# Hybrid decoder trunk on one core: pool mixer features moved directly behind the keys, memory sums queued later, one accumulator bank of the values in another pool

## The chip, the core and the metric

The kernel runs on one core of a Trainium2 chip. The metric is the device time of one execution in microseconds, the median of several runs. The core has a matrix engine (TensorE, PE in the rows), VectorE (DVE), ScalarE (ACT), GpSimd (POOL), SyncE (SP), whose queue issues most of the transfers, and 16 DMA engines. Each engine works through its own queue in order, and engines meet at semaphores.

## What is computed

One decoder layer for 256 tokens of width 2048, all in float32:

- a mixer on the normalized input `h`: eight heads of a gated DeltaNet (width 1024) beside a multi-scale pool mixer (width 1024), both out of one projection `p = h @ w_in`, then an output projection;
- cross-attention into 256 memory tokens, with keys and values from `mem_h @ w_xkv`;
- a gated MLP with a causal convolution, and a final norm.

The pool mixer, of which this is about, is short:

```python
for i, w in enumerate((2, 4, 8, 16)):           # four groups of 256 features
    mean = (running sum of u over the last w positions) / min(position, w)
    groups.append(mean - u)
y = einsum('bsng,ngh->bsnh', stack(groups), w_pool) * pool_scale
```

The DeltaNet takes q, k, v, z out of the same projection (q, k, v through a causal convolution of 4 taps and SiLU), builds for each head and each half of the tokens a triangular matrix from the keys, inverts it, and runs two chunks of 128 tokens through the state.

## The kernel before

Activations are kept transposed (features on partitions, 256 tokens along the row). Every float32 product is made of three: weights and activations are split in a high and a low part (`split`, lines 100 to 102: ScalarE copies the high part, VectorE subtracts), and high x high, high x low and low x high are accumulated. `gemm_part` (lines 132 to 146) does one feature tile of 128 outputs with 16 pairs of matmuls, one of 512 columns and one of 256.

`unit` (line 126) gives a gemm its weights: `load_raw` fetches 1 MB on SP's queue into one of three `raw` buffers, and `wsplit` splits it in two halves, each into one of four `whi` and `wlo` buffers. So the split of weights can run two gemms ahead of TensorE.

**Order of the work.** The text of the kernel is not the order of the engines: a planner sorts the instructions by the place in the text and by its own reckoning of when each is ready, and keeps the dependencies. `tc.issue_after(x)` ties what is written inside to come behind `x` on the engine of `x`. Side work is written as generators in lanes. `pump(anchor)` is called three times in each gemm (line 145, behind k-tiles 4, 9 and 15); it advances every lane by one step and ties that step's matmuls behind the gemm's own matmul. The lanes are "dn" (decays, four key pairs, inverses), "dp" (the four delta pairs, one after the other), "pool" (outputs of the pool groups) and "mem" (the memory tokens).

The stage around the change, lines 640 to 839, in the order of the text:

1. eight key features `in_k` with their convolution (lines 640 to 648); behind each second one a `key_pair` joins lane "dn"; then `inverses`;
2. four pairs p = 0 to 3 of heads (lines 651 to 666): two q, two v, two z projections; q and v go through `conv_feature` (evacuation, a scaling on GpSimd at line 347, one ScalarE step at 349, three VectorE steps at 351), then `delta_pair(p)` joins lane "dp"; behind pair 1 the lane "mem" gets `memory()`;
3. four pool groups (line 667): `pool_group` (lines 580 to 607) loads `w_pool[n]`, splits it, does two projections `in_u`, scales each on GpSimd (592), sums windows on GpSimd with n+1 additions (598), forms the mean on VectorE (602 to 605), splits it into `mx`, and queues `pool_out` (567 to 579), which waits 6+n steps and then multiplies by the weights and writes rows of yT;
4. sixteen memory keys `kk` (830 to 839). Behind key 0 lane "mem" is drained, behind key 8 lanes "dn", "dp" and "pool", and `memory_sums` (674 to 694) joins lane "ms": for two thirds of the memory features sums and differences of the token halves, split into `mS`, needed by the memory values;
5. the memory values (`values`, 696 to 825), a Strassen-like scheme with seven products b1 to b7, each in a bank of PSUM. Two pools of banks serve this stage: `psg` with three (the gemms') and `psd` with four.

`inverses` (390 to 451): it sends the key matrices U through DRAM (393, 397) into a layout W of 16x16 blocks, inverts those by 15 times two VectorE steps on V (404, 406), sends V through DRAM into Yall (408, 411), waits 20 steps, and then does for each pair two rounds of a doubling (`Z` on VectorE at 420, `qp` on TensorE two steps later at 425, `pp` two steps later at 432, the subtraction from Yall at 433) and a last round.

`delta_pair` (453 to 565): after SiLU and transposes it waits until the inverse of its pair is done (495), then `wps`, the state, `cps` (520), R on VectorE (524), two steps later `w` (531), then the outputs `ops` (539), their statistics, and five steps later the transposes `otp` (560). Pair 3 has extra waiting steps (`more`).

The steps that the rows name are these lines:

```python
for l in range(2):                                    # inverses
    Z = st4("Z", "sq"); dve.transpose(Z, Y[p]); yield; yield
    pe.matmul(qp[:, j], C[:, j], Z[:, j], ...)         # 425
while not inv_done[p]: yield                           # delta_pair, 495
dve.tensor_tensor(am, mg[:, :, 0], mg[:, :, 1], ALU.add)   # memory_sums, 682
```

Of the kernel before, what the change touches and what calls it, by code (L numbers as in the profile page):

```python
# [10 lines left out]
F32 = mybir.dt.float32  # L11
F32R = mybir.dt.float32r
AF = mybir.ActivationFunctionType
ALU = mybir.AluOpType
# [3 lines left out]
P = 128  # L18
D = 2048
T = 256  # L20
M = 256
KT = D // P
# [20 lines left out]
def hybrid_trunk(ctx, tc, a, out):  # L43
    nc = tc.nc
    act, dve, pool, pe = nc.scalar, nc.vector, nc.gpsimd, nc.tensor
# [3 lines left out]
    psg = pre.enter_context(tc.tile_pool(name="psg", bufs=3, space=bass.MemoryType.PSUM))  # L49
    psd = pre.enter_context(tc.tile_pool(name="psd", bufs=4, space=bass.MemoryType.PSUM))  # L50
# [4 lines left out]
    def big(name, shape, dt):  # L55
        return per.tile(shape, dt, name=name, tag="big", bufs=3)

    def ev(name, n=T):
        return per.tile([P, n], F32, name=name, tag="ev", bufs=4)
# [29 lines left out]
    def pv(k, i=None, j=None):  # L89
        s, e = PRM[k]  # L90
        if i is None:
            return prm[:, s:e]
        return prm[:, s + i:s + (i + 1 if j is None else j)]

    def cv(k):
        s, e = CST[k]
        return cst[:, s:e]


    def split(hi, lo, src):  # L100
        act.copy(hi, src)  # L101
        return dve.tensor_tensor(lo, src, hi.bitcast(F32), ALU.subtract)  # L102
# [10 lines left out]
    last_split = [None]  # L113
# [18 lines left out]
    def gemm_part(ps, u, src, k0, n, tot):  # L132
        i = None
        for k in range(n):
            kk = k0 + k
            h, l = u(k)
            xt = src(kk)
            full = xt.rearrange("p s t -> p (s t)")
            if kk == tot - 1:
                pe.matmul(ps[:, T:], l, xt[:, 0, :], start=False, stop=False)  # L140
                i = pe.matmul(ps, h, full, start=False, stop=True)
            else:
                pe.matmul(ps, h, full, start=kk == 0, stop=False)  # L143
                i = pe.matmul(ps[:, T:], l, xt[:, 0, :], start=False, stop=False)  # L144
            if kk % 16 in (4, 9, 15):
                pump(i)
# [51 lines left out]
    with tc.tile_pool(name="dn", bufs=1, reuse_waits="tile") as dn:  # L198
# [35 lines left out]
        for c in range(4):  # L234
# [5 lines left out]
            if c % 2 == 1:  # L240
                g = c // 2
# [325 lines left out]
        def pool_out(n, mx, wp):  # L567
            for _ in range(6 + n):
                yield
            for o_ in range(2):  # L570
                wu = lambda k: (wp[:, 0, k, o_ * P:(o_ + 1) * P], wp[:, 1, k, o_ * P:(o_ + 1) * P])
                ps = psd.tile([P, 512], F32, name="pool", tag="d")
                gemm_part(ps, wu, lambda k: mx[k], 0, 2, 2)
                f = n * 2 + o_
                c = ev("pc")
                act.activation(c, ps[:, T:], AF.Copy, scale=pv("pool_scale", f))
                yt = ev("py")
                dve.scalar_tensor_tensor(yt, ps[:, :T], pv("pool_scale", f), c, ALU.mult, ALU.add)
                split(yT[:, f, 0, :], yT[:, f, 1, :], yt)

        def pool_group(n):
            wpr = load_raw(a["w_pool"][n], [P, 2, 256], "wp")
            wp = dn.tile([P, 2, 2, 256], F32R, name="wp", tag="u4", bufs=2)
            split(wp[:, 0], wp[:, 1], wpr)
            mx = [dn.tile([P, 2, T], F32R, name="mx", tag="C", bufs=2) for _ in range(2)]
            for c in range(2):
                f = n * 2 + c
                ps = gemm([unit(a["w_in"][f], "wi")], hsrc, [KT], "in_u")
                m = evac(ps, "u")
                A = dn.tile([P, T + 16], F32, name="pA", tag="xp", bufs=3)  # L590
                pool.memset(A[:, 0:16], 0.0)
                pool.tensor_tensor(A[:, 16:], m, rxb, ALU.mult)
                src = A
                for l in range(n + 1):
                    s = 1 << l
                    lo = 2 * s - 1
                    B = dn.tile([P, T + 16], F32, name="pB", tag="xp", bufs=3)
                    pool.tensor_tensor(B[:, lo:], src[:, lo:], src[:, lo - s:T + 16 - s], ALU.add)
                    src = B
                w = 2 << n  # L600
                mt = ev("mt")
                dve.scalar_tensor_tensor(mt, src[:, 16:], 1.0 / w, A[:, 16:], ALU.mult, ALU.subtract)
                m16 = dn.tile([P, 16], F32, name="m16", tag="m16", bufs=1)
                dve.tensor_tensor(m16, src[:, 16:32], cv("inv")[:, n * 16:(n + 1) * 16], ALU.mult)
                dve.tensor_tensor(mt[:, 0:16], m16, A[:, 16:32], ALU.subtract)
                split(mx[c][:, 0, :], mx[c][:, 1, :], mt)
            job("pool", pool_out(n, mx, wp))
# [39 lines left out]
            if h % 2 == 1:  # L647
                job("dn", key_pair(h // 2))
        job("dn", inverses())
        yT = None  # L650
        for p in range(4):
            q2, v2, z2 = (dn.tile([P, 2, T], F32, name=n, tag=n, bufs=b) for n, b in (("q2", 2), ("v2", 1), ("z2", 2)))
            for nm, fb, comp, dst in (("q", 8, 0, q2), ("v", 24, 2, v2)):
                for i in range(2):
                    h = 2 * p + i
                    ps = gemm([unit(a["w_in"][fb + h], "wi")], hsrc, [KT], "in_" + nm)
                    conv_feature(ps, comp, h, dst[:, i, :], "c" + nm)
            for i in range(2):
                ps = gemm([unit(a["w_in"][32 + 2 * p + i], "wi")], hsrc, [KT], "in_z")
                m = evac(ps, "z")  # L660
                pool.tensor_tensor(z2[:, i, :], m, rxb, ALU.mult)
            if yT is None:
                yT = big("yT", [P, KT, 2, T], F32R)
            job("dp", delta_pair(p, q2, v2, z2))
            if p == 1:
                job("mem", memory())
        for n in range(4):
            pool_group(n)
        mT = mbox[0]


# [2 lines left out]
        def memory_sums():  # L674
            for g in range(2):
                tmp = dn.tile([P, 2, 4, T], F32, name="mtmp", tag="kall", bufs=1)
                place = (("Dm0", "Dm1", "Dm2", "Dm3"), ("q2", "q2", "z2", "z2"))[g]
                s = [dn.tile([P, 2, T], F32R, name="mS", tag=n, bufs=1 + g) for n in place]
                mS.append((s[:2], s[2:]))
                am, ss = tmp[:, 0], tmp[:, 1].rearrange("p w (k t) -> p w k t", k=2)  # L680
                mg = mT[:, 4 * g:4 * g + 4]
                dve.tensor_tensor(am, mg[:, :, 0].bitcast(F32), mg[:, :, 1].bitcast(F32), ALU.add)
                yield
                a11, a12, a21, a22 = (am[:, k:k + 2, t * P:(t + 1) * P] for t in range(2) for k in (0, 2))
                s5, s6, s7, s3 = (ss[:, w] for w in range(4))
                dve.tensor_tensor(s5, a21, a22, ALU.subtract)
                dve.tensor_tensor(s7, a11, a21, ALU.subtract)
                yield
                dve.tensor_tensor(s6, a11, s5, ALU.subtract)
                dve.tensor_tensor(s3, a12, s6, ALU.subtract)  # L690
                yield
                for w in range(2):
                    split(s[w], s[2 + w], tmp[:, 1, 2 * w:2 * w + 2])
                yield

        def values():
# [74 lines left out]
            def multiply(c, kind, h, uses):  # L771
                hi, lo = ready.pop((c, kind, h))
                g = int(kind[1]) if kind[0] in "ul" else h
                for name, stat in uses:
                    begins = (c, name) not in bk
                    if begins:
                        pool_, tag = (psg, "g") if name in ("b7", "b2") else (psd, "d")
                        bk[c, name] = pool_.tile([P, 512], F32, name="pvs", tag=tag)
                    ends = h == 1 and ENDS[name] == kind
                    ps = bk[c, name]  # L780
                    for i in range(2):
                        xh, xl = stat(g, i)
                        seq(pe.matmul(ps, xh, hi[:, i], start=begins and i == 0, stop=False, skip_group_check=True))  # L783
                        seq(pe.matmul(ps, xh, lo[:, i], start=False, stop=False, skip_group_check=True))
                        seq(pe.matmul(ps, xl, hi[:, i], start=False, stop=ends and i == 1, skip_group_check=True))  # L785
# [88 lines left out]
    r2, _, r2run = rnorm(sq2, "r2", False)  # L874
# [315 lines left out]
    for s in range(-AHEAD, len(plan)):  # L1190
# [13 lines left out]
        b, k = s // NS, s % NS  # L1204
# [52 lines left out]
    for m, (k, c) in enumerate(steps):  # L1257
# [4 lines left out]
        n = blocks.index(k // 4)  # L1262
# [122 lines left out]
```

## Time and profile before

| | |
|---|---|
| median of three runs | 1519.69 us (1519.25 to 1519.73) |
| the profiled execution | 1517.59 us |
| its span, first to last instruction | 1515.8 us |
| TensorE busy | 98% of the span |
| VectorE, ScalarE, GpSimd busy | 75%, 57%, 15% |
| mean granted TensorE clock | 0.994 |

The span of the stage in question goes from about 77 us (end of the keys) to about 410 us (end of the memory keys); the values follow to about 490 us, and then the output projection, the attention and the MLP, which the change does not touch. A row of the trace says who waited for whom; "idle" is the time in which the engine did nothing ahead of the instruction. Matmuls are pipelined: one of 512 columns is listed with some 0.39 us but the next starts about 0.23 us behind it, so a full TensorE shows as busy without holes.

### The profile page before, as it was taken

How to read it: one execution, taken by the hardware profiler on the slowest of the kernel's cores; microseconds unless marked ns; L12 is line 12 of the kernel's file. 1: busy time of each engine (PE TensorE's matmuls, PEld its weight loads, DVE VectorE, ACT ScalarE, POOL GpSimd, SP SyncE). 2: the span in 40 equal slices, each digit the busy share in tenths (PEclk: the TensorE clock that was granted, in tenths of full speed). 3: DMA queues.
4: the chain of work that ended last, by engine and by line, in shares of the span. 5: the costliest groups of instructions: out<-in, count | busy, mean ns of one | idle time of the engine just before them, and what ended most of it. 6: DMA issues, size and time to landing. Idle time of an engine off the chain costs nothing.

```text
span 1515.8 us, 20595 instructions
## 1 busy us (share of the span) xinstructions
PE 1479.2 (98%) x7698; PEld 1253.6 (83%) x7698; DVE 1137.3 (75%) x1489; ACT 870.9 (57%) x1265; POOL 230.6 (15%) x249
## 2 busy tenths in 40 slices
PE   7899999999999999999999999999999999999997
PEld 5788889888877888998888888888888887888885
DVE  6878887677688776666767898889889998455445
ACT  6565666554466544555656766666666766444433
POOL 0432523442100121000322000000000000000000
PEclk9999999999999999999999999999999999999999
DMA  7345443455476655434569988888888879765651
GB/s 269 123 172 189 142 171 126 144 183 208 157 232 222 249 191 176 163 139 139 195 197 344 285 243 248 256 264 257 266 270 270 247 200 363 242 194 190 196 185 56
DMA packets 74933, 317.07 MB, mean 209 GB/s; under 512 B 12240, under 2 KB 12624, under 8 KB 59728
## 3 DMA queue, kind: packets, MB, share of 16 engines
q1 hardware_dynamic: 67136, 287.96, 54.1%
q0 software_dynamic: 7552, 27.27, 9.6%
q8 instruction: 60, 0.98, 0.3%
q10 hardware_dynamic: 144, 0.52, 0.1%
q14 instruction: 41, 0.34, 0.1%
HBM read 306.15 MB, written 9.57 MB: 208 GB/s over the span
## 4 chain that ended last, share of the span: by engine, by line
PE 81%; DVE 8%; ACT 4%; POOL 3%; DMA 3%; issue 2%; SPq 0%; POOLq 0%; DVEq 0%; ACTq 0%
PE b L1028 10%; PE b L1030 10%; PE b L1029 10%; PE acc L1246 5%; PE acc L1247 5%; PE acc L1248 5%; PE xq L143 4%; PE mix L143 4%; PE xo L143 3%; PE kk L143 3%; PE xq L144 2%; PE mix L144 2%; PE xo L144 2%; PE pvs L783 2%; PE pvs L785 2%
## 5 line engine op out<-in xcount | busy, mean ns | idle before, releaser
L1111 ACT CAST wh<-wr 128x1024 fp32r<-128x1024 f32 x162 | 168.4, 1050 | 87.5 <-DVE wr L1147 30.2
L1112 DVE TENSOR_TENSOR wl<-wr,wh 128x1024 fp32r<-128x1024 f32 x162 | 194.7, 1218 | 26.3 <-ACT wh L1111 25.1
L1028 PE MATMUL b<-wh,hP 128*128 128x512 f32 x484 | 190.8, 395 | 2.4 <-DVE xres L853 2.4
L1030 PE MATMUL b<-wh,hP 128*128 128x512 f32 x484 | 190.3, 394 | 0.0
L1029 PE MATMUL b<-wl,hP 128*128 128x512 f32 x484 | 188.8, 390 | 0.0
L1112 DVE TENSOR_TENSOR wl<-wd,wh 128x1024 fp32r<-128x1024 f32 x88 | 107.5, 1224 | 102.8 <-ACT wh L1111 102.7
L1111 ACT CAST wh<-wd 128x1024 fp32r<-128x1024 f32 x88 | 92.7, 1054 | 118.5 <-PE acc L1248 114.6
L1246 PE MATMUL acc<-wh,aring 128*128 128x512 f32 x320 | 124.5, 389 | 0.0
L1248 PE MATMUL acc<-wh,aring 128*128 128x512 f32 x320 | 124.5, 389 | 0.0
L1247 PE MATMUL acc<-wl,aring 128*128 128x512 f32 x320 | 124.5, 389 | 0.0
L1111 ACT CAST wh<-ring 128x1024 fp32r<-128x1024 f32 x80 | 83.2, 1051 | 53.6 <-PE b L1030 29.4
L1112 DVE TENSOR_TENSOR wl<-ring,wh 128x1024 fp32r<-128x1024 f32 x80 | 96.7, 1218 | 21.4 <-ACT wh L1111 21.4
L102 DVE TENSOR_TENSOR wil<-wi,wih 128x1024 fp32r<-128x1024 f32 x78 | 99.9, 1287 | 15.8 <-ACT wih L101 15.4
L1028 PEld LDWEIGHTS b<-wh,hP 128*128 128x128 f32 x484 | 91.0, 188 | 21.6 <-issue 2.7
L1030 PEld LDWEIGHTS b<-wh,hP 128*128 128x128 f32 x484 | 90.9, 188 | 18.5
L1029 PEld LDWEIGHTS b<-wl,hP 128*128 128x128 f32 x484 | 91.0, 188 | 18.0
L1144 POOL DMA_DIRECT2D ring<-in_w_gu x40 | 34.6, 865 | 379.4 <-DVE sg L1078 365.2
L101 ACT CAST wih<-wi 128x1024 fp32r<-128x1024 f32 x78 | 81.4, 1049 | 17.2 <-DMA wi<-in_w_in 6.3
L143 PE MATMUL xq<-h2T,wqh 128*128 128x512 f32 x240 | 84.9, 393 | 0.0
L143 PE MATMUL kk<-mT,wkh 128*128 128x512 f32 x240 | 84.5, 393 | 0.0
L143 PE MATMUL xo<-oT,woh 128*128 128x512 f32 x240 | 84.3, 392 | 0.0
L143 PE MATMUL mix<-yT,wmh 128*128 128x512 f32 x240 | 84.1, 392 | 0.0
(500 smaller groups left out, 3825.9 us busy)
## 6 DMA issues: line engine op xcount, KB each, us to landing
wr<-in_w_gu SPq DMA_DIRECT2D x158, 512.0 KB, 7.0
wd<-in_w_down SPq DMA_DIRECT2D x88, 512.0 KB, 4.8
wi<-in_w_in SPq DMA_DIRECT2D x39, 1024.0 KB, 4.9
ring<-in_w_gu POOLq DMA_DIRECT2D x40, 512.0 KB, 7.3
wk<-in_w_k SPq DMA_DIRECT2D x16, 1024.0 KB, 4.9
wm<-in_w_mix SPq DMA_DIRECT2D x16, 1024.0 KB, 5.0
wq<-in_w_xq SPq DMA_DIRECT2D x16, 1024.0 KB, 4.9
wo<-in_w_xo SPq DMA_DIRECT2D x16, 1024.0 KB, 4.9
```

The source lines that it names most:

```text
L101: act.copy(hi, src)
L102: return dve.tensor_tensor(lo, src, hi.bitcast(F32), ALU.subtract)
L143: pe.matmul(ps, h, full, start=kk == 0, stop=False)
L144: i = pe.matmul(ps[:, T:], l, xt[:, 0, :], start=False, stop=False)
L1028: pe.matmul(ps, xh, wh, start=first and i == 0, stop=False, skip_group_check=True)
L1029: pe.matmul(ps, xh, wl, start=False, stop=False, skip_group_check=True)
L1030: m = pe.matmul(ps, xl, wh, start=False, stop=last and i == 1, skip_group_check=True)
L1111: cast[:] = [put(act.copy(h, src))]
L1112: less[:] = [put(dve.tensor_tensor(l, src, h.bitcast(F32), ALU.subtract))]
L1246: pe.matmul(acc[t, n], ah, wh, start=first, stop=False)
L1247: pe.matmul(acc[t, n], ah, wl, start=False, stop=False)
L1248: return pe.matmul(acc[t, n], al, wh, start=False, stop=last)
```

## The change

Three edits. The four pool groups go ahead of the pairs, with yT allocated ahead of them; their buffers move to tags that the pairs use later (`wp` in two tiles under the tags of q2 and z2, two buffers each, in place of one tile under `u4`; `mx` under the tags of R and vs, one buffer each, in place of two under `C`). The first operation of each half of the memory sums is tied behind the split of weights that was traced last. The accumulator b6 of the values comes from pool `psg` in place of `psd`.

```diff
@@ pool_out
-                wu = lambda k: (wp[:, 0, k, o_ * P:(o_ + 1) * P], wp[:, 1, k, o_ * P:(o_ + 1) * P])
+                wu = lambda k: (wp[0][:, k, o_ * P:(o_ + 1) * P], wp[1][:, k, o_ * P:(o_ + 1) * P])
@@ pool_group
-            wp = dn.tile([P, 2, 2, 256], F32R, name="wp", tag="u4", bufs=2)
-            split(wp[:, 0], wp[:, 1], wpr)
-            mx = [dn.tile([P, 2, T], F32R, name="mx", tag="C", bufs=2) for _ in range(2)]
+            wp = [dn.tile([P, 2, 256], F32R, name="wp", tag=g, bufs=2) for g in ("q2", "z2")]
+            split(wp[0], wp[1], wpr)
+            mx = [dn.tile([P, 2, T], F32R, name="mx", tag=g, bufs=1) for g in ("R", "vs")]
@@ the stage
         job("dn", inverses())
-        yT = None
+        yT = big("yT", [P, KT, 2, T], F32R)
+        for n in range(4):
+            pool_group(n)
         for p in range(4):
...
-            if yT is None:
-                yT = big("yT", [P, KT, 2, T], F32R)
             job("dp", delta_pair(p, q2, v2, z2))
             if p == 1:
                 job("mem", memory())
-        for n in range(4):
-            pool_group(n)
@@ memory_sums
-                dve.tensor_tensor(am, mg[:, :, 0].bitcast(F32), mg[:, :, 1].bitcast(F32), ALU.add)
+                with tc.issue_after(last_split[0].ins):
+                    dve.tensor_tensor(am, mg[:, :, 0].bitcast(F32), mg[:, :, 1].bitcast(F32), ALU.add)
@@ values, multiply
-                        pool_, tag = (psg, "g") if name in ("b7", "b2") else (psd, "d")
+                        pool_, tag = (psg, "g") if name in ("b7", "b2", "b6") else (psd, "d")
```

## Rows read from the trace of the kernel before

**Rows 1.** The page, part 1: engine, busy us (share of the span), instructions.
```profile
PE 1479.2 (98%) x7698; PEld 1253.6 (83%) x7698; DVE 1137.3 (75%) x1489; ACT 870.9 (57%) x1265; POOL 230.6 (15%) x249
```

**Rows 2.** Waits of TensorE: us in total, times, longest us.
```profile
PE gps L313 <- DVE gg L306: 3.0, 1, 3.0
PE qp L425 <- DVE Z L420: 2.7, 2, 1.5
...
PE w L531 <- DVE R L524: 2.5, 2, 1.4
...
PE otp L560 <- DVE o L554: 2.4, 1, 2.4
PE in_k L143 <- ACT wih L101: 1.4, 1, 1.4
...
PE pvs L783 <- DVE KV L799: 0.5, 2, 0.3
```

**Rows 3.** Windows: the header names the columns; gemms 1 to 8 are 76.6:128.4.
```profile
core 0: us, PE busy (x) PEld busy (x) DVE busy (x) ACT busy (x) POOL busy (x), PEclk, DMA share, GB/s
40.00:50.00 10.00, 7.27 (x42) 6.11 (x41) 9.27 (x30) 4.73 (x9) 3.98 (x6) 1.00 0.28 105
50.00:60.00 10.00, 9.75 (x47) 8.36 (x48) 9.37 (x21) 5.12 (x9) 3.11 (x3) 0.83 0.34 114
76.60:128.40 51.80, 51.80 (x324) 46.38 (x323) 40.71 (x91) 30.14 (x72) 18.60 (x19) 1.00 0.52 171
145.00:350.00 205.00, 197.33 (x1271) 174.33 (x1270) 157.69 (x288) 122.55 (x276) 81.61 (x90) 1.00 0.44 157
252.00:311.00 59.00, 59.00 (x381) 52.62 (x381) 41.47 (x91) 36.32 (x87) 22.47 (x29) 1.00 0.40 136
```

**Rows 4.** Timeline of TensorE: start us, us, instruction [idle before, released by].
```profile
150.07 1.13 PE L425 MATMUL qp<-Z,C 128*128 128x128 f32 x8 [1.11 <-DVE Z L420]
...
161.42 1.13 PE L425 MATMUL qp<-Z,C 128*128 128x128 f32 x8 [1.55 <-DVE Z L420]
...
191.07 0.46 PE L531 MATMUL w<-R,Yall 128*128 128x128 f32 x2 [1.40 <-DVE R L524]
...
320.97 0.49 PE L531 MATMUL w<-R,Yall 128*128 128x128 f32 x2 [1.10 <-DVE R L524]
...
343.46 0.92 PE L560 MATMUL otp<-cst,o 128*128 128x128 f32 x4 [2.37 <-DVE o L554]
```

**Rows 5.** Timeline of VectorE: first, two middle and last of V's steps.
```profile
121.96 0.17 DVE L404 SCALAR_TENSOR_TENSOR tmp<-V,W 128x15 f32<-128x15 f32 x1
...
125.19 0.73 DVE L406 TENSOR_TENSOR V<-V,tmp 128x60 f32<-128x60 f32 x1
...
130.60 0.22 DVE L406 TENSOR_TENSOR V<-V,tmp 128x60 f32<-128x60 f32 x1
...
135.59 0.18 DVE L406 TENSOR_TENSOR V<-V,tmp 128x15 f32<-128x15 f32 x1
```

**Rows 6.** Timeline of SP's queue: V's way back from DRAM.
```profile
139.70 3.77 SPq L411 DMA_DIRECT2D Yall<-vscr  x8
```

**Rows 7.** Timeline of VectorE: what stands ahead of the late steps.
```profile
160.18 0.47 DVE L106 SCALAR_TENSOR_TENSOR mT<-mraw,prm,mT 128x256 fp32r<-128x256 f32 x1
...
187.25 3.41 DVE L351 SCALAR_TENSOR_TENSOR q<-cqxp,prm,q 128x256 f32<-128x256 f32 x6
...
317.75 1.22 DVE L682 TENSOR_TENSOR mtmp<-mT 128x1024 f32<-128x1024 f32 x1
...
319.15 1.50 DVE L102 TENSOR_TENSOR wkl<-wk,wkh 128x1024 fp32r<-128x1024 f32 x1
...
338.10 1.21 DVE L682 TENSOR_TENSOR mtmp<-mT 128x1024 f32<-128x1024 f32 x1
```

**Rows 8.** DMA issues: count, KB each, median us from issue to landing.
```profile
wp<-in_w_pool SPq DMA_DIRECT2D x4, 256.0 KB, 2.9
```

**Rows 9.** Timeline of GpSimd: the scaling of a q feature beside V.
```profile
125.11 0.74 POOL L347 TENSOR_TENSOR cqxp<-cqm,rxrb 128x256 f32<-128x256 f32 x1 [5.93 <-DVE cqm L160]
```

**Rows 10.** Groups of GpSimd, 84 to 345 us: count, busy us, mean ns, idle before.
```profile
L598 POOL TENSOR_TENSOR pB<-pB 128x269 f32<-128x269 f32 x6 | 3.8, 635 | 0.5
```

## The prediction

> **What bounds the kernel now.** I read the page first: TensorE is busy 98% of the span [rows 1], so a change of order that leaves the matmuls alone can only win back TensorE's idle time, or add to it. Next I read TensorE's waits [rows 2]. In the stretch that the change reorders (from the last key feature to the first third of the memory keys) three lines wait: the inverses' `qp` (2.7 us, twice), the delta pairs' `w` (2.5, twice) and `otp` (2.4, once), 7.6 us together. The other long waits (`gps` and its kind) lie ahead of the change or far behind it. So this change is worth 7.6 us at most, 0.5% of the run, plus fractions of a microsecond. About 0.2%, 3.04 us, is what a measurement of this kernel can tell from no change. A wait can also cost more than its length: `gps` waits 3.0 us in the slice 40 to 50, and in the slice behind it the granted clock averages 0.83 [rows 2, 3], a time at the lower of the two levels (1.2 of 2.4 GHz); 17% of 10 us is 1.7 us. The five waits of the stretch are 1.10 to 2.37 us long [rows 4] and lie where the clock is at its upper level [rows 3].
>
> **What moves, counted in pumps.** Lanes advance one step at each of three matmuls per projection, so I number pumps from the end of the keys, three to a gemm, and count yields. The inverses' first real step, `Z` of pair 0, is pump 33, its `qp` pump 35, the second `qp` 39, and pair p's inverse is done at 45+12p: lane "dn" alone sets these, before and after. What runs beside them changes. Before: pairs at gemms 1 to 24, pool features at 25 to 32, memory at pumps 37 to 62; delta pairs end at 56, 70, 84 and 109. After: pool features at gemms 1 to 8, pairs at 9 to 32, memory at pumps 61 to 86; delta pairs start at 43, 61, 79 and 97 and end at 57, 75, 93 and 122. Every pair now finds its inverse done, and pair 3 ends inside memory key 8, just ahead of the drain there, which therefore has nothing to force. The sums start at pump 124 in both.
>
> **The waits one by one**, each from the row before it:
>
> First `qp`, 1.11 us [rows 4]. `Z` needs the inverses' V, which goes through DRAM; V's last step is at 135.59 and SP issues the way back from 139.70 on for 3.77 us [rows 5, 6]. After, the conv features of pairs 0 and 1 no longer run beside V, but pool features do. Bounds: 1.11 gained, or all of rival 2 lost. I take 0.6 gained, the half, because the pool features bring other work.
>
> Second `qp`, 1.55 us [rows 4]. `Z` stands behind a memory split (`mT`, 160.18) and a weight split on VectorE [rows 7]. After, pump 39 is in pair 0 and the memory starts 22 pumps later. Gained: 1.55 (bounds 0 and 1.55).
>
> `w` of pair 0, 1.40 us [rows 4]: R waits behind six conv steps that took 3.41 us [rows 7], in the memory's time. After, this step is pump 51, without memory. Gained: 1.40 (bounds 0 and 1.40).
>
> These two can come back where the memory now runs: beside pairs 2 and 3, inverses 2 and 3 and the deltas of pairs 1 and 2, much the same mix. Bounds: nothing, or both in full, 2.95 us. I take half, 1.5 lost.
>
> `w` of pair 3, 1.10 us [rows 4]. Ahead of R, VectorE did the first operation of the memory sums (1.22 us at 317.75) and between the two R's a weight split of 1.50 [rows 7]. The sums' text comes 24 pumps later, but the planner pulled the operation forward as soon as `kall` was free. The change queues it behind the last weight split traced at pump 124, and R is then at pump 109: it cannot come first. Gained: 1.10 (bounds 0 and 1.10; the split may still stand there).
>
> `otp`, 2.37 us [rows 4]: the sums' second operation (1.21 us at 338.10) stands ahead of the statistics that `otp` needs [rows 7]. After, sums start 2 pumps behind `otp`. Their cost is 1.21, and the rest of the wait is GpSimd's and VectorE's queue. Gained: 2.37 less 0.5 that I leave for that queue (bounds 1.21 and 2.37). Who waits for the sums: `22` of the values, 15 pumps or more behind; cover of that length hides their delay, and without it their four splits would show.
>
> Weights in the pool stage. The four `w_pool` loads (256 KB, 2.9 us to landing [rows 8]) move up on SP past 24 weight loads, and each holds one of three raw buffers until group n-2 has left its `wp` buffers; at the same time SP carries the inverses' trips through DRAM. In the old place SP was free of these. Nothing waits in gemms 1 to 8 now: TensorE is busy 51.80 of 51.80 us [rows 3]. Nearest row: the one wait of a projection for a weight, 1.4 us [rows 2]. Bounds 0 and 1.4; I take 0.5, since the split buffers hold two gemms. The two `memT` loads go back on SP with the memory, beside the same kind of loads as now: nothing.
>
> Edits at nothing: the new tags. `mx` had two buffers and has two, `wp` two and two; the pair's q2 needs group 2's `wp`, read at pump 28, and is written behind gemm 9 (pump 27) after GpSimd's step; R and vs are wanted from pump 45, eight behind the last pool output. Bank b6 from one pool to the other: the projections' pool has three banks, b2 and b7 take two, the third was evacuated with the last memory key. The wait of the values, 0.5 us in two [rows 2], is for a read of b7 and stays (bounds: 0.5 either way).
>
> **Sum.** 0.6 + 1.55 + 1.40 + 1.10 + 1.87 = 6.5 gained; 1.5 + 0.5 = 2.0 lost; net 4.5. The profiled execution took 1517.59 (span 1515.8 and 1.8 around it) and would take 1513.1. The median of the runs is 2.1 above it, 1519.69, so I forecast **1515.2**. With every gain at its upper bound and no loss it is 7.6 less, 1512.1.
>
> **Rival 1: the waits follow the memory.** All three early waits (1.11 + 1.55 + 1.40 = 4.06) are VectorE's queue, and it is the memory with a conv stage that fills it. Then they return in pairs 2 and 3, and only 1.10 + 1.87 - 0.5 = 2.5 us is won: 1517.2, within 0.2%. For it: the same work meets the same chains. Against it: the pairs no longer wait for their inverse, so two of the chains have lost their neighbours.
>
> **Rival 2, on the other side: pool features stop V.** A step of V takes 0.22 us, but the one at 125.19 took 0.73 and ended with the GpSimd operation that had begun at 125.11 and took 0.74 [rows 5, 9]. Undisturbed, eight features hold GpSimd for 8 x 0.74 and 20 sums of 0.635 [rows 9, 10]: 18.6 us in eight gemms, where the eight projections now there have 8 x 0.74 = 5.9. VectorE is already busy 40.71 of 51.80 us there [rows 3], against 41.47 of 59.00 us in the pool features' present place with the deltas. Groups 2 and 3, which meet V, have 14 sums and four scalings in four gemms, 8.9 and 3.0 us, 11.9 of half the 51.80: 46%. If V's 13.8 us (121.96 to 135.77 [rows 5]) stretch by that share, 6.3 us, `qp` waits 1.1 + 6.3 = 7.4 us where I left 0.5, and the clock falls, 1.7: -4.5 + (7.4 - 0.5) + 1.7 = 4.1 slower, 1523.8. It decides from the point where V ends so late that its way back (7.7 us from V's last step to the last of the eight issues [rows 5, 6], and the landing) ends behind pump 33. Against it: keys' U may reach V earlier, as ScalarE no longer waits for conv features ahead of it, and four more pool outputs lie before that pump.
> The Trainium skill (SBUF — State Buffer, section Who interferes with whom) states the rule: a VectorE instruction with two SBUF inputs and a GpSimd instruction that reads SBUF exclude each other for their whole length. By that rule every pool sum that meets a step of V holds it up to the sum's end, and the time is this rival's; the row of 0.73 agrees with it for one pair of operations, and how many pairs meet no run here shows yet.
>
> **A rival that I exclude:** that the change does not do what it says. Text order binds the matmuls (each lane step is tied to a matmul), and the sums to a split; only VectorE's and ScalarE's order around them is free, and that is rival 1.
>
> **Chances.** Forecast 0.59, rival 1 0.26, rival 2 0.15. So faster 0.59, same 0.26, slower 0.15. The range goes from 1511.0 (all gains, 1512.1, and one more for what the bounds leave out) to 1522.0, which takes in rival 1 and the milder half of rival 2, where V is late by 4 us and not 6.
>
> **What would show it.** Right: no `qp` wait in the first two steps; `w` and `otp` out of TensorE's waits around the memory keys; the sums' additions behind key 9; delta pair 3 ending in key 8; at most 2 to 3 us of waits in pairs 2 and 3 with `mT` in front. Rival 1: `qp` or `w` waits of 1 to 1.5 us there. Rival 2: V's steps of 0.6 us and more, a first `qp` wait of over 4 us, a slice with a lower clock behind it. Wrong altogether: a new wait in gemms 1 to 8, where TensorE has none now, or a wait for weights there over 1.4 us; or a difference behind 490 us, where nothing is edited.

## The result and the profile after

The changed kernel takes 1534.83 us (median, 1531.85 to 1536.15) where the kernel before took 1519.71: ratio 1.0099 [1.0087, 1.0111], 15.0 us slower. The forecast was 1515.2 with a range from 1511.0 to 1522.0: wrong in sign. The profiled execution of after took 1534.20 us, span 1532.4, against 1515.8 before: 16.6 us to account for.

The page of after, part 1 (it answers to [rows 1]): TensorE has the same 7698 matmuls and is busy 9.5 us longer.

```profile
PE 1488.7 (97%) x7698; PEld 1261.5 (82%) x7698; DVE 1136.5 (74%) x1489; ACT 873.8 (57%) x1265; POOL 227.5 (15%) x249
```

**Where it went.** The last matmul of a projection is line 141; its start times in the timeline of TensorE, before and after, cut the run in stages (gemms are counted from the end of the keys, as in the prediction):

| last matmul of | before | after | after behind by | won or lost in the stage |
|---|---|---|---|---|
| gemm 6 | 115.30 | 116.98 | 1.7 | |
| gemm 9 | 133.98 | 144.01 | 10.0 | +8.4 |
| gemm 12 | 152.91 | 170.59 | 17.7 | +7.7 |
| gemm 24 | 251.94 | 270.43 | 18.5 | +0.8 |
| gemm 32 | 311.06 | 332.16 | 21.1 | +2.6 |
| last memory key | 410.31 | 426.67 | 16.4 | -4.7 |

Behind the memory keys nothing changes. So after falls 16 us behind in the six gemms from 7 to 12. A stage also holds the side matmuls that were moved into it: by their rows, gemms 7 to 12 hold 1.0 us more of them after than before (two pool outputs, 1.4 us each, came in), and the stage of the memory keys 1.0 us less. The rest is waits and slower matmuls. The waits of TensorE after (to be held against [rows 2]; us in total, times, longest):

```profile
PE qp L425 <- DVE Z L420: 8.4, 2, 5.6
...
PE in_q L143 <- ACT wih L101: 2.7, 1, 2.7
...
PE qp L444 <- ACT Zc L440: 2.2, 1, 2.2
PE in_q L144 <- DVE wil L102: 2.0, 1, 2.0
...
PE in_u L144 <- DVE wil L102: 0.8, 1, 0.8
```

`w` and `otp` are gone from the list, as forecast. New are waits of `in_q` and `in_u` for their weights, and `qp` has grown from 2.7 to 8.4. The windows of after show the granted clock where these waits lie (columns as in [rows 3]: the last but two is the granted clock):

```profile
131.00:144.00 13.00, 8.31 (x35) 6.59 (x34) 12.12 (x29) 6.42 (x10) 6.65 (x8) 0.74 0.44 156
...
157.00:171.00 14.00, 8.28 (x40) 7.14 (x40) 9.63 (x15) 5.72 (x9) 3.77 (x5) 0.78 0.54 171
171.00:232.00 61.00, 58.76 (x384) 52.29 (x383) 41.60 (x74) 36.45 (x80) 15.34 (x19) 0.97 0.37 130
232.00:290.00 58.00, 55.20 (x359) 49.68 (x359) 45.37 (x76) 35.70 (x83) 27.33 (x29) 0.97 0.40 135
```

**Gemms 7 to 9.** The timeline of TensorE, from the end of gemm 8 on:

```profile
131.14 0.39 PE L141 MATMUL in_u<-hT,wih 128*128 128x512 f32 x1
134.27 0.79 PE L143 MATMUL in_q<-hT,wih 128*128 128x512 f32 x1 [2.74 <-ACT wih L101]
137.01 0.58 PE L144 MATMUL in_q<-hT,wil 128*128 128x256 f32 x1 [1.95 <-DVE wil L102]
137.40 0.63 PE L143 MATMUL in_q<-hT,wih 128*128 128x512 f32 x1
137.82 0.41 PE L144 MATMUL in_q<-hT,wil 128*128 128x256 f32 x1
...
141.00 0.28 PE L144 MATMUL in_q<-hT,wil 128*128 128x256 f32 x1
141.11 0.40 PE L143 MATMUL in_q<-hT,wih 128*128 128x512 f32 x1
```

Two waits in a row, and behind them matmuls of 0.63 us and 0.41 us that take 0.40 and 0.28 from 141 us on: the lower of the two clock levels (1.2 of 2.4 GHz). With 0.31 and 0.76 at `in_u` of gemm 7 the idle time is 5.76 of the 8.4 us; the rest, some 3 us, are the slower matmuls. Who held `wih` up is read in the timeline of ScalarE:

```profile
130.05 0.41 ACT L101 CAST mx<-mt 128x256 fp32r<-128x256 f32 x1 [3.84 <-DVE mt L605]
...
132.87 0.40 ACT L101 CAST yT<-py 128x256 fp32r<-128x256 f32 x1 [0.95 <-DVE py L578]
133.18 2.93 ACT L101 CAST wih<-wi 128x1024 fp32r<-128x1024 f32 x3
```

The cast of a pool feature (`mx`) stands at the head of ScalarE's queue for 3.84 us, waiting for VectorE's `mt`; the weights of gemm 9, cast at 133.18, are behind it and behind the casts of a pool output (`yT`). VectorE's timeline goes one step further back, and shows V too (compare [rows 5]):

```profile
129.24 0.43 DVE L602 SCALAR_TENSOR_TENSOR mt<-pB,pA 128x256 f32<-128x256 f32 x1 [2.77 <-POOL pB L598]
...
130.27 0.16 DVE L404 SCALAR_TENSOR_TENSOR tmp<-V,W 128x15 f32<-128x15 f32 x1
...
133.65 0.74 DVE L406 TENSOR_TENSOR V<-V,tmp 128x48 f32<-128x48 f32 x1
...
146.91 0.43 DVE L602 SCALAR_TENSOR_TENSOR mt<-pB,pA 128x256 f32<-128x256 f32 x1 [2.92 <-POOL pB L598]
...
152.97 0.18 DVE L406 TENSOR_TENSOR V<-V,tmp 128x15 f32<-128x15 f32 x1
...
166.82 0.71 DVE L420 STREAM_TRANSPOSE Z<-Yall 128x512 f32<-128x512 f32 x1 [0.26 <-issue]
```

`mt` in turn waits at the head of VectorE's queue for GpSimd's window sums (`pB`). V's first step stands behind that `mt`: it starts 8.3 us later than before (130.27 against 121.96), and V ends 17.4 us later (152.97 against 135.59). **Gemms 10 to 12** then lose 7.7: the first `qp` comes at 167.68 behind 5.58 us of idle where it waited 1.11, and its eight matmuls take 2.04 us where they took 1.13 [rows 4].

```profile
167.68 2.04 PE L425 MATMUL qp<-Z,C 128*128 128x128 f32 x8 [5.58 <-DVE Z L420]
```

V's lateness is not all of that wait. The last issue of its way back began at 162.3 and such an issue lands 1.9 us behind, so `Yall` was there at some 164.2 (an estimate from these rows), but `Z` ran at 166.82, directly behind the convolution of a value on VectorE (1.51 us from 165.04). So some 2 us of the 5.58 are VectorE's queue once more.

SP's queue has a share as well. The loads go one to a gemm; counted in order, the one for gemm 7 left SP at 94.27 before and leaves at 109.50 after, 15.2 us later, with a `w_pool` load ahead of it that takes one of the three raw buffers:

```profile
96.73 0.33 SPq L110 DMA_DIRECT2D wi<-in_w_in  x1
104.09 0.33 SPq L110 DMA_DIRECT2D wp<-in_w_pool  x1
109.50 0.33 SPq L110 DMA_DIRECT2D wi<-in_w_in  x1
```

**Pairs 1 and 2** wait 2.24 us (`qp` of line 444) and 2.80 (of line 425) where the memory now runs. In both, a value's convolution stands ahead of the inverse's step, waiting for GpSimd's scaling: on ScalarE `v` in front of `Zc` for the first, on VectorE `v` in front of `Yall` and `Z` for the second.

```profile
224.89 0.51 ACT L349 ACTIVATE v<-cvxp,prm 128x256 f32<-128x256 f32 x1 [2.35 <-POOL cvxp L347]
225.30 0.35 ACT L440 COPY Zc<-zp 64x256 f32<-64x256 f32 x1
```

```profile
278.29 0.48 DVE L351 SCALAR_TENSOR_TENSOR v<-cvxp,prm,v 128x256 f32<-128x256 f32 x1 [1.17 <-ACT v L349]
278.69 0.68 DVE L433 TENSOR_TENSOR Yall<-Yall,pp__2827 128x512 f32<-128x512 f32 x1
```

So three theories stood for the 16 us. **Queues:** pool work that waits for GpSimd's sums stands at the heads of VectorE's and ScalarE's queues, with weight casts and V behind it. **Shared memory:** rival 2, the sums stop the steps of V themselves. **Ring:** the pool weights hold raw buffers, so projection weights land late.

### The profile page after: what moved, and what is told of

It reads as the page before. It is cut to its first block, busy times and chain, and to the rows that moved or that the text cites. A ratio compares the mean times of both kernels' runs of the same rounds, so it can differ in the third digit from the quotient of the medians.

```text
span 1532.4 us, 20582 instructions
## 1 busy us (share of the span) xinstructions
PE 1488.7 (97%) x7698; PEld 1261.5 (82%) x7698; DVE 1136.5 (74%) x1489; ACT 873.8 (57%) x1265; POOL 227.5 (15%) x249
## 4 chain that ended last, share of the span: by engine, by line
PE 85%; DVE 6%; POOL 3%; ACT 3%; issue 2%; DMA 1%; SPq 0%; DVEq 0%; POOLq 0%; ACTq 0%
PE b L1027 10%; PE b L1029 10%; PE b L1028 10%; PE acc L1245 5%; PE acc L1246 5%; PE acc L1247 5%; PE xq L143 4%; PE kk L143 4%; PE mix L143 4%; PE xo L143 3%; PE xq L144 2%; PE kk L144 2%; PE mix L144 2%; PE xo L144 2%; PE pvs L782 2%; PE pvs L783 2%
## 5 line engine op out<-in xcount | busy, mean ns | idle before, releaser
L1111 DVE TENSOR_TENSOR wl<-wr,wh 128x1024 fp32r<-128x1024 f32 x162 | 195.0, 1220 | 26.7 <-ACT wh L1110 25.4
L1029 PEld LDWEIGHTS b<-wh,hP 128*128 128x128 f32 x484 | 91.3, 189 | 18.7
```

Source lines behind the costliest of these rows:

```text
L1029: m = pe.matmul(ps, xl, wh, start=False, stop=last and i == 1, skip_group_check=True)
L1111: less[:] = [put(dve.tensor_tensor(l, src, h.bitcast(F32), ALU.subtract))]
```

## The experiments

The time of each is the median of its runs. The ratio is to the kernel before, run on the same chip; differences in us between versions are differences of ratios times 1519.7 us.

**The later sums alone** (before, with that part of the change):

```
+                with tc.issue_after(last_split[0].ins):
                     dve.tensor_tensor(am, mg[:, :, 0]..., mg[:, :, 1]..., ALU.add)
```

> The kernel before with the second edit alone: the first operation of each half of the memory sums is tied behind the last split of weights. By the prediction this takes away the wait of 1.10 us at w of pair 3 and most of the 2.37 us at otp: 1.5 to 3.0 us faster, 1516.7 to 1518.2. Rival: another instruction of VectorE takes the place of the sums' operation ahead of R and of the statistics, the waits stay and the time is within 1 us of 1519.7.

Measured: 1514.79 us, 0.9965 [0.9951, 0.9978], 5.3 us faster. `otp` is out of TensorE's waits, and `w` falls from 2.5 to 1.8; `qp` rises from 2.7 to 4.1:

```profile
PE qp L425 <- DVE Z L420: 4.1, 2, 2.5
...
PE w L531 <- DVE R L524: 1.8, 2, 1.4
```

The part works, by more than expected and more than its waits explain: the profiled execution, the slowest of its seven runs (1515.92), has a span only 1.7 us shorter than before's, and the rest of the gain has no row. The longer `qp` is the first one, with 2.50 us where it waited 1.11, although VectorE does the same work there in the same order; in the next run, whose edit does not reach that stage either, it does not wait at all. So this wait differs from one execution to the next by more than the 0.6 us that the forecast hoped to win at it.

**The bank alone** (before, with `"b6"` added to the names that take the other pool):

> The kernel before with the third edit alone, b6 out of the gemms' banks. By the prediction nothing changes: 1519.7 within 0.5, the 0.5 us of waits at the values stays. Rival: the bank is wanted by the output projection or by a later product and the values or the first gemm behind them lose 1 us or more.

Measured: 1519.18 us, 0.9997 [0.9986, 1.0007]: nothing.

**The move without the later sums** (after, with that wait taken out):

```
-                with tc.issue_after(last_split[0].ins):
-                    dve.tensor_tensor(am, ...)
+                dve.tensor_tensor(am, ...)
```

> The changed kernel without the later queueing of the memory token sums, so that of the three parts the move of the pool features and the bank are left. If the parts add up, the sums were worth 3.7 to 5.3 us (run alone) and this is 1538 to 1540 us, with the wait of otp for o (2.4 us) and that of w in pair 3 back. If the late sums are themselves what holds the queue heads in pairs 1 and 2 of the changed kernel (the qp waits of 2.2 and 2.8 us there), this is no slower than the changed kernel, 1531 to 1535 us.

Measured: 1534.27 us, 1.0097 [1.0081, 1.0113]: the same as after. The parts don't add up. `w` and `otp` are out of TensorE's waits here too. The sums did not get out of their way: in the timeline of VectorE the first operation of each half stands directly ahead of R and of the statistics (line 549), as in the kernel before [rows 7]:

```profile
360.39 1.21 DVE L680 TENSOR_TENSOR mtmp<-mT 128x1024 f32<-128x1024 f32 x1
361.53 0.34 DVE L524 SCALAR_TENSOR_TENSOR R<-cps,negA,R 128x128 f32<-128x128 f32 x1
...
379.08 1.21 DVE L680 TENSOR_TENSOR mtmp<-mT 128x1024 f32<-128x1024 f32 x1
380.22 0.15 DVE L549 TENSOR_TENSOR f<-f,ssq 128x4 f32<-128x4 f32 x1
```

What no longer stands there is the pool stage. In the kernel before, VectorE waited 3.58 us for GpSimd's window sums just ahead of the first of these operations, and 2.51 us behind R (at 323.42):

```profile
315.62 0.43 DVE L602 SCALAR_TENSOR_TENSOR mt<-pB,pA 128x256 f32<-128x256 f32 x1 [3.58 <-POOL pB L598]
```

I read it so: the sums cost TensorE something only together with the pool work in the same queue, and with that gone there was nothing left for the second part to do. The loss of after is the move's, with the tags that come with it.

**No window sums** (after; the 20 `pool.tensor_tensor(B, ...)` left out, `src` stays `A`):

> The changed kernel without GpSimd's 20 window sums (the mean is taken of the feature itself, so that part of the pool mixer is left out). Theory of the queues: in the changed kernel the mean of each feature stands in VectorE's queue and its cast in ScalarE's until GpSimd has scaled and summed, and the casts of weights and V's first step stand behind them; without the sums each of these heads comes 0.6 to 2.9 us earlier, so most of some 8 us at gemms 7 to 9 and most of the 5.6 us at the first qp with its slow clock go: 1520 to 1525. Theory of the locks: only the six or so steps of V that took 0.64 to 0.74 us come back to 0.22, about 3 us off the qp wait, gemms 7 to 9 stay: 1530 to 1532. Theory of the raw buffers: the weights land as late as now, gemms 7 to 9 keep their 8 us: 1527 or more.

Measured: 1523.5 us, 1.0033 [1.0018, 1.0048], so 10 us of the loss go with the sums. V runs from 125.92 to 143.51. TensorE's waits:

```profile
PE qp L425 <- DVE Z L420: 6.1, 2, 3.3
...
PE in_q L144 <- DVE wil L102: 1.7, 1, 1.7
...
PE in_q L143 <- ACT wih L101: 0.7, 1, 0.7
```

The sums are behind most of it, but this run can't tell queues from shared memory. It changes what is computed, so it shows where the time goes and is no version to use.

**The sums on VectorE** (after):

```
-                    pool.tensor_tensor(B[:, lo:], ...)
+                    dve.tensor_tensor(B[:, lo:], ...)
```

> The changed kernel, with the 20 window sums on VectorE and not on GpSimd. The work is kept and the hand-over between the two engines goes. Queue theory: the wait of the copy of the mean for GpSimd (2.8 us) goes and with it the cast of the features behind it, gemms 7 to 9 lose 3 to 5 us where they lost 8.5; VectorE itself has some 10 us more to do in those gemms, so V starts no earlier than about 128 us, and the first qp wait stays at 3 to 5 us: 1524 to 1530 us. Shared-memory theory (what costs is that VectorE and GpSimd hold each other up while GpSimd sums): the steps of V all fall to about 0.25 us, V takes about 14 us, but gemms 7 to 9 keep their loss: 1529 to 1532 us. If VectorE's own load decides: 1534 us or more.

Measured: 1527.57 us, 1.0054 [1.0040, 1.0069], 6.8 us better than after by the ratios. The time is what the queue theory gave, but not by its way: `in_q` still waits 2.7 and 3.3 us, and V still takes 21 us (129.14 to 150.26). What the run does settle is what the sums do to V's own steps, rival 2's mechanism. The 30 steps of V in the groups by line (VectorE, 110 to 160 us), first in after, then here:

```profile
L406 DVE TENSOR_TENSOR V<-V,tmp 128x15 f32<-128x15 f32 (+7 forms) x15 | 4.6, 304 | 0.2
L404 DVE SCALAR_TENSOR_TENSOR tmp<-V,W 128x15 f32<-128x15 f32 (+7 forms) x15 | 4.4, 291 | 0.2
```

```profile
L404 DVE SCALAR_TENSOR_TENSOR tmp<-V,W 128x15 f32<-128x15 f32 (+7 forms) x15 | 3.5, 233 | 0.0
L406 DVE TENSOR_TENSOR V<-V,tmp 128x15 f32<-128x15 f32 (+7 forms) x15 | 3.5, 233 | 0.0
```

9.0 us against 7.0, and 7.1 before (7.7 in the run without the sums). GpSimd's sums cost V's own steps 2.0 us at most, where V became 9.1 us longer (22.9 against 13.8). The other 7 us are other instructions between the steps: `mt`, `mx`, `wp`, `py`, and the idle time of 0.77 and 2.92 us ahead of `mt`. The other direction no run settles: GpSimd's scaling of a feature (`pA`), which the sums wait for, took 1.65 us at 125.42 beside a weight split of VectorE, and a scaling of the same size (`cqxp`) 0.73 us at 150.48. So some 0.9 us of a wait for the sums (1.65 less 0.73, an estimate) may be shared memory.

**Buffers of their own for the pool weights** (after):

```
-            wpr = load_raw(a["w_pool"][n], [P, 2, 256], "wp")
+            wpr = dn.tile([P, 2, 256], F32, name="wpr", tag="C", bufs=2)
+            nc.sync.dma_start(wpr, a["w_pool"][n])
```

> The changed kernel, with the pool weights loaded into two buffers of their own and not into the ring of raw buffers that the projections' weights use. Ring theory (the pool weights hold raw buffers, so that the projection weights of gemms 7 to 9 land late): those gemms lose some 8.5 us in the changed kernel, of which 5 to 8 us come back, 1526 to 1530 us, and the two waits of in_q for its weights (2.7 and 2.0 us) go. Queue theory (the casts of weights that have already landed stand behind pool work that waits, at the head of the queues of VectorE and ScalarE): nothing that can be measured, 1532 to 1536 us, both waits stay above 1.5 us. A part of each would show as 1 to 4 us.

Measured: 1528.4 us, 1.0061 [1.0046, 1.0075], 5.8 us better than after. The wait for `wih` goes, as the ring theory has it. The waits for the low half don't go, they spread over gemms 9 to 11 (1.06, 2.41 and 2.13 us by the timeline):

```profile
PE qp L425 <- DVE Z L420: 5.0, 3, 2.8
PE in_q L144 <- DVE wil L102: 3.5, 2, 2.4
...
PE in_v L144 <- DVE wil L102: 2.1, 1, 2.1
```

So the weights are there in time now and are cast late on VectorE, which idles 12.7 us ahead of `mt` in this run. Both theories hold a part, one behind the other. The stages tell them apart. Cut by the same start times as the table above, gemms 7 to 9 took 18.7 us before and 27.0 after. They take 19.5 with buffers of their own, although `mx` still stands 3.84 us at the head of ScalarE's queue, 20.9 without the sums, but 27.7 with the sums on VectorE, where `mx` waits 3.12. What is lost in these gemms needs late weights and a stalled queue head together; taking GpSimd out of the sums alone gave nothing back there.

**The inverse seven pumps later** (after, 27 waiting steps ahead of the first inverse for 20):

```
-            for _ in range(20):
+            for _ in range(27):
```

> The changed kernel with 27 waiting steps in the inverses in place of 20, so the first qp stands some 14 us later on TensorE. If V's lateness alone makes that wait, 5.6 us and the slow clock behind it (2 us) go and gemms 7 to 9 keep their 8 us: 1527 to 1529. If Z is late for another reason (VectorE's queue around it), the wait follows it and the time stays near 1534.8. Pair 0 then waits for its inverse about five steps, for which no matmul waits.

Measured: 1520.09 us, 1.0010 [1.0000, 1.0020], 13.5 us better than after, 7 better than expected. TensorE waits for the weights as in after (2.8 and 1.9 us), V is as late as in after (129.68 to 152.37), yet the first `qp` no longer waits, nor does `qp` in pair 2, and the one of line 444 is small:

```profile
PE in_q L143 <- ACT wih L101: 2.8, 1, 2.8
...
PE in_q L144 <- DVE wil L102: 1.9, 1, 1.9
...
PE qp L444 <- ACT Zc L440: 0.6, 1, 0.6
```

Gemms 7 to 9 keep their loss (27.0 us), and small waits come at other steps (`pp` of line 449 1.0, `zp` 0.5): 8.2 us of waits in the stretch (gemm 1 to the last memory key), where before had 7.5. The expectation counted the first wait alone. The same shift moves the steps of all four inverses, so I read the two later waits as a matter of which step met which queue head.

**Two mends together, then three.** After with the later inverse and the own buffers:

> The changed kernel with both mends together: the pool weights in buffers of their own and 27 waiting steps ahead of the first inverse. If the ring's loss and the lateness of the first inverse are two losses, the two gains add (6 us and 13 us): 1513 to 1516 us. If the run with buffers of its own only moved the loss from the gemms 7 to 9 to VectorE's queue in the gemms 9 to 11 (its waits of in_q and in_v for the low half of the weights, 5.6 us together), so that what it won was the first qp wait, which the later inverse takes away as well: 1518 to 1521 us, no better than the later inverse alone, with those waits still at 4 to 6 us.

Measured: 1520.8 us, 1.0010 [1.0000, 1.0019], the same as the later inverse alone. As the second case had it, 4.3 us (`in_q`) and 2.1 us (`in_v`) of waits for the low half are left:

```profile
PE in_q L144 <- DVE wil L102: 4.3, 3, 2.4
...
PE in_v L144 <- DVE wil L102: 2.1, 2, 1.4
```

After with the later inverse and the sums on VectorE, the ring as in the change:

> The changed kernel with the 20 window sums on VectorE and 27 waiting steps ahead of the first inverse, but the pool weights in the ring of raw buffers as the change has them. If the ring of raw buffers has a loss of its own (the projection weights of gemms 7 to 9 land late and are cast late, whatever the sums do): in_q still waits 5 to 6 us for its weights, and 1518.5 to 1521 us, some 5 us above the run with all three. If the sums alone were the matter: 1513 to 1516 us, as the run with all three.

Measured: 1521.13 us, 1.0015 [1.0004, 1.0025]: nothing either. The ring's loss stands alone (26.7 us in gemms 7 to 9), 2.2 and 3.3 us of waits:

```profile
PE in_q L144 <- DVE wil L102: 3.3, 1, 3.3
...
PE in_q L143 <- ACT wih L101: 2.2, 1, 2.2
```

After with all three:

> As the run before it, and the 20 window sums on VectorE. If what is left in the gemms 9 to 11 is VectorE standing at the head of its queue for GpSimd's sums (12.7 us of idle time between 110 and 160 us in the run with buffers of its own): the waits for the low half fall below 2 us in all, 1513 to 1516 us, 3 to 5 us better than without. If it is VectorE's load there (some 9 us of sums more): the same or worse, 1518 to 1523 us.

Measured: 1514.05 us, 0.9966 [0.9957, 0.9976], 5.2 us faster than before. No wait of `in_q` is left; two of `in_v`, 2.1 us together:

```profile
PE in_v L144 <- DVE wil L102: 2.1, 2, 1.1
```

On top of the later inverse, neither the buffers nor the sums bring anything, and both together bring 6.7 us (1.0010 to 0.9966). Weights that land late and a VectorE that stands still are two obstacles on one path: with one taken away, the other ends last. With all three, gemms 7 to 9 take 18.1 us, no more than before, and the waits of the stretch come to 4.5 us.

**A try for more** (the later sums alone, with 23 waiting steps):

> The kernel before with the memory token sums queued later, as in the run of that part alone, and with 23 waiting steps ahead of the first inverse where there were 20, so that each step of the four inverses comes one gemm later. If the two qp waits that are left there (4.1 us together) are only a matter of when the steps are due: they go, and 1510.5 to 1513 us, against 1514.8 for the part alone. If what is late is the work in VectorE's queue whatever the step (the wait moves with the step): 1514 to 1516 us.

Measured: 1515.53 us, 0.9977 [0.9966, 0.9988], not better than the later sums alone. The two long `qp` waits go; waits of 0.8 (for GpSimd's `mraw`) and 0.8 us (for `mt`) come at other `qp`. With 1.4 at `rmpb` and 1.0 at `pp` the waits of the stretch come to 4.2 us, against 6.2 with the later sums alone; the two medians can't show a difference of that size.

So two versions beat the kernel before by the same 0.35%: the part of the change that queues the sums later, alone, and the whole change with its three mends.

## Why the prediction was wrong

Of the five waits that the forecast counted (7.5 us by the rows) four are gone from their places; the first `qp` grew. With what came new the stretch has 16.8 us of waits: 5.8 for weights, 5.6 at the first `qp`, 5.0 in pairs 1 and 2 and 0.4 for the memory's statistics (`rmpb`), with a lower clock behind the longest. The forecast left 3.1 us: 7.6 less 6.5, and 2.0 of new ones.

**"Weights in the pool stage", 0.5 (bounds 0 and 1.4): the step that failed first.** Gemms 7 to 9 lost 8.4. The text named the ring of raw buffers, and the run with own buffers showed it to be real. But it took the price from the longest wait of a projection for a weight in the kernel before, and it argued that "nothing waits in gemms 1 to 8 now". The stage was 100% busy before and lost 8.4 us all the same: busy time says nothing of how much lead the weights have. And the step looked at SP alone: it did not ask what stands ahead of the weight casts on ScalarE and VectorE, where the rows of after show `mx` and `mt` waiting for GpSimd at the heads. The kernel before showed such heads in the old place of the pool features (3.58 and 2.51 us on VectorE, above).

**The first `qp`, 0.6 gained.** Measured: idle 5.58 us, where 0.5 was left, and gemms 10 to 12 fell back by 7.7 in all. That was rival 2's outcome in kind (it had a `qp` wait of 7.4 and a fall of the clock). Its deciding point held: V's way back ended behind pump 33. Its mechanism did not: it had the sums stop V's steps for 6.3 us, and they did for 2.0 at most. V started 8.3 us late and was drawn out by 7 us more because it shares an in-order queue with work that waits. The reading of the row before was off as well: `Z` ran at 149.22, directly behind a weight split and a value's convolution on VectorE, when the last issue of V's way back had ended at 143.47 and such an issue took 2.1 us to land. That wait was the queue's, not the way through DRAM. The Trainium skill (SBUF — State Buffer, section Who interferes with whom) states that a VectorE instruction with two SBUF inputs and a GpSimd instruction that reads SBUF exclude each other. The rows agree with it: steps of 0.2 us took up to 0.74 beside GpSimd's scaling and sums, and with the sums on VectorE the 30 steps took no longer than before (7.0 and 7.1 us). The 6.3 us that I had worked out do not agree with the rows: they stretched all of V by GpSimd's busy share, and only six of the 30 steps took 0.64 us or more.

**Returns beside the memory, 1.5 (bounds 0 and 2.95).** Pairs 1 and 2 waited 2.24 and 2.80 us, 5.0, with a clock of 0.97 in both windows. The kind was right, at other steps (both at `qp`, none at `w`) and behind other work (a value's convolution, not `mT`), and the upper bound was too low: it was the sum of the old waits, not the length of the queue that could form. With the later inverse most of it is gone.

**Second `qp` and `w` of pair 0, 2.95 gained:** right, both are gone from their places.

**`w` of pair 3 and `otp`, 2.97 gained:** both are gone (4.7 us are won behind gemm 32: these two waits, 3.5, and 1.0 of side matmuls that moved away), but not for the reason given. I gave it to the later queueing of the sums. In the run without that the sums stand where they stood and neither step waits; what the move took away was VectorE's wait for GpSimd ahead of them. In the kernel before, the later queueing alone wins 5.3 us by its ratio, where I forecast 4.5 for the whole change.

**Tags and bank, 0:** the bank right by its own run. The tags were not tried alone; the first step that writes `q2` began at 151.47, 0.3 us behind its scaling (0.73 us from 150.48), so this buffer at least held nothing up.

What bounded the range on the slow side was rival 2 in its milder half. I set rivals for V and for the memory separately, each with its own price, and none in which they share a cause: one stalled queue head delays weight casts, V and, in part through V, the inverses.

## What to carry to other kernels

When work moves to a new stage, list for each in-order queue there which of the moved instructions will wait for another engine, and what critical work stands behind it: a stage whose matrix engine is 100% busy may live on a few microseconds of lead. Price a wait at the length of the chain that feeds its queue head, not at waits seen in the kernel before, and add the clock behind it. Where a mend does nothing, try it together with another before giving it up: two obstacles on one path hide each other.

## What was not expected of the hardware

A gap of 2.74 us and one of 1.95, with a single matmul between them, were followed by matmuls of 0.63 us instead of 0.39 up to 140.6 us; one of 5.58 by a `qp` that took 2.04 instead of 1.13: the lower clock level, in windows with a granted clock of 0.74 and 0.78. Before the change, waits of 1.1 to 2.4 us in this stretch left the clock at 1.00 [rows 3, 4]. The length of a wait alone does not tell: the same wait of 2.8 us at the `qp` of pair 2 was followed by a `qp` of 1.72 us in after, 1.56 and 2.04 with the buffers of their own and without the sums, and 1.13 with the sums on VectorE and without the later sums. Of the 16 us in gemms 7 to 12, idle time that was not there before is 10.2 (5.76 in gemms 7 to 9, and 5.58 less 1.11 behind them) and side matmuls are 1.0; the clock of the two windows, 0.74 of 13 us and 0.78 of 14, takes up to 0.26 x 13 + 0.22 x 14 = 6.5 us, enough for the other 4.8.
